# Where the heads' queries, keys and values are loaded in an attention period: loads with places of their own, SP's order written out, products placed later

## The chip, the cores and the metric

One core of a Trainium2 chip runs the kernel. The metric is device time in microseconds for one execution. The engines are TensorE (PE in the rows; its weight loads are PEld), VectorE (DVE), ScalarE (ACT), GpSimd (POOL) and SyncE (SP). SP does no arithmetic; it issues DMA transfers, and so does ScalarE here. A `q` behind an engine's name is its sequencer, which waits and issues.

## The reference, cut to what matters

One layer of a hybrid decoder, in float32: RMSNorm, one input projection, three groups of heads, a gate, an output projection, a residual and a last RMSNorm. The change touches the attention of the prompt, 2048 positions:

```python
for win, dil in ((128, 1), (512, 4), (2048, 16)):      # 8 heads of 64
    s = q @ k / 8 - slope * dil * dist                 # inside the dilated window
    p = exp(s - max(s)); l = sum(p); o = p @ v / l
attn_o = merge of the three o, weighted by their denominators
mem_o  = softmax(mq @ mk / 8) @ mv                     # 4 heads, 256 memory tokens
```

The kernel takes one maximum per position and head over all three windows, so that the three sums and products can be added up without a further weighting.

## The kernel before, in words

Queries and keys were projected earlier and lie in scratch memory as a high and a low part (`dq_hi`, `dq_lo`, `dk_hi`, `dk_lo`), so that float32 products are made of exact pieces. Values lie in the output `p_v`.

The attention is a chain of twelve units: eight `Head`s (0 to 7) and four `MemHead`s. Each has two halves. `scores` loads the unit's keys (`ks`, two loads of 512 KB) and queries (`qh`, `ql`, four loads of 512 KB, `q_load`) and, for a `Head`, its values in three layouts (`v1`, `v2`, `v3`, 512 KB each). It then makes the score blocks in 24 steps (six for a memory head): two products of `qk` per block on TensorE, the bias added on the way out of PSUM by VectorE (`biased`, L791), maxima by `mx.add` (L735). ScalarE regroups the keys by residue before steps 0 and 16 (`regroup`, `kr`, L814). The score tiles are S3, SS (also called S1) and S2.

`Maxima.finish(half)` ends each half of the maxima. TensorE transposes them (L742), VectorE reduces (`mc`, L744), a DMA stores 4 KB to the scratch `dmax` (L745), and a second one loads them back, spread over 128 partitions, as one half of `Rm`, 512 KB (L746). The load must wait until the store has landed. Both DMAs go out on ScalarE's queue. `finish(0)` is called at step 22 of a head's `scores`, `finish(1)` in its `values`.

`values` subtracts Rm from the scores on GpSimd (L911, L912, L917, L932, L933), takes exponentials on ScalarE (L913, L914, L918, L934, L936), multiplies by the values on TensorE into `acc` (`pv`, L906), and sums the weights (`Sums.add`, L759). `finish_head` turns the sums into reciprocals, spreads them with two groups of transposes (L771, L780; `rx`, L774), multiplies `osb` by them (L781) and stores it to `dmix` (L784, two stores of 256 KB).

`period` runs the scores of unit i+1 beside the values of unit i. `values` is a generator that yields places: a place p is taken at the first step k with k/24 not below p, a place above 1.0 in the next period. `with tc.manual_schedule(engines={PE})` keeps TensorE's program order as written in the seven periods of full heads; the order on the other engines, SP's queue among them, is found by the planner of the framework, which starts an instruction when it believes it ready and lets `high_priority(350)` go ahead of others. So in the kernel before the loads, written at the head of `scores`, are issued when the planner finds their buffer free.

Buffers: keys, queries and values of a unit lie in pools `keys[turn]` and `vals[turn]`, by the unit's parity, one set each. Those of turn 1 take the place of the rows and weights of the projection (`p0`), which `z_last`, the last of the gate's projection, runs with beside unit 0's scores. PSUM banks are shared by rings: `psP` 0 and 1, `psQ` 2 and 3 (scores), `psT` 4 and 5 (transposes).

Of the kernel before, what the change touches and what calls it, by code (L numbers as in the profile page):

```python
# [8 lines left out]
F = mybir.dt.float32  # L9
R = mybir.dt.float32r  # L10
# [9 lines left out]
T = 2048  # L20
NS = 32
NR = T + NS
H = 8
# [4 lines left out]
SLOPE = [2.0 ** -(h + 1) for h in range(H)]  # L28


def f32(ap):
    return ap.bitcast(F)


def ap_of(x, off, dims):
    return bass.AP(tensor=x.tensor, offset=x.offset + off, ap=dims)
# [238 lines left out]
def tile_step(ctx, tc, x_prompt, x_sample, mem_prompt, ck, cv, cconv, cmk, cmv, g_in, w_in, conv_w,  # L275
              g_mem, w_mem, w_out, g_final,
              y_p, y_s, p_k, p_v, p_cv, p_mk, p_mv, s_k, s_v, s_cv):
    nc = tc.nc
# [18 lines left out]
    psP, psQ, psT = Ring((0, 1)), Ring((2, 3)), Ring((4, 5))  # L297
# [5 lines left out]
    dk_hi = dr.tile([512, T], F, name="dk_hi")  # L303
# [393 lines left out]
    def z_last():  # L697
        for ct in range(8 - ZL, 8):
            yield from z_proj(ct, "A")
# [21 lines left out]
    parts_ = [None, None]  # L721
    dmax = [dr.tile([64, 32], F, name="dmax%d" % i) for i in range(2)]

    class Maxima:


# [10 lines left out]
        def finish(self, half):  # L737
            sl = slice(32 * half, 32 * half + 32)
            m = wk.tile([128, 32], F, name="mx")
            nc.vector.tensor_reduce(m, self.parts[:, sl, 0:self.n], axis=AX.X, op=OP.max)  # L740
            pt = psT.tile([128, 4, 128], F, name="pt")
            nc.tensor.transpose(pt[:32, 0], m, ident)  # L742
            mc = wk.tile([32, 32], F, name="mc")
            nc.vector.tensor_reduce(mc, pt[:32, 0].rearrange("p (q c) -> p c q", q=4), axis=AX.X, op=OP.max)  # L744
            nc.scalar.dma_start(self.d[sl], mc)  # L745
            nc.scalar.dma_start(self.Rm[:, 1024 * half:1024 * half + 1024], ap_of(self.d, 1024 * half, [[0, 128], [1, 1024]]))  # L746

    class Sums:

# [12 lines left out]
    def finish_head(o_sb, sums, row, at):  # L762

        rx = wk.tile([128, 16, 64], F, name="rx", bufs=1)
        ls = rx[:, 0:8].rearrange("p (a b) c -> p a (b c)", a=4)
        nc.scalar.activation(ls.rearrange("p a (J b) -> p a J b", b=8),
                             sums.ps.rearrange("p x y -> p (x y)").rearrange("p (J a b) -> p a J b", a=4, b=8), AF.Copy)
        yield at
        pt = psP.tile([128, 4, 128], F, name="pp")
        for a in range(4):  # L770
            nc.tensor.transpose(pt[:, a], ls[:, a], ident)  # L771
        rl = wk.tile([128, 16], F, name="rl")
        nc.vector.reciprocal(rl.rearrange("p (a g) -> p a g", g=4), pt[:, :, 0::32])
        nc.scalar.activation(rx, rl.unsqueeze(2).to_broadcast([128, 16, 64]), AF.Copy)  # L774
        for k in range(2):
            yield at + 0.06 + 0.03 * k
            pb = psP.tile([128, 4, 128], F, name="pp")
            for i in range(4):
                c = 8 * k + 2 * i
                nc.tensor.transpose(pb[:, i], rx[:, c:c + 2].rearrange("p a e -> p (a e)"), ident)  # L780
            nc.vector.tensor_mul(o_sb[:, 4 * k:4 * k + 4], o_sb[:, 4 * k:4 * k + 4], pb)  # L781
        for g in range(2):
            dst = dmix[row:row + 64, :T].rearrange("p (r g b) -> p g r b", g=2, b=128)[:, g]
            nc.sync.dma_start(dst, o_sb[g * 64:(g + 1) * 64])  # L784
# [8 lines left out]
    class Head:  # L793


        def __init__(self, h, turn):
            self.h, self.turn = h, turn

        def scores(self):
            h, sl = self.h, -SLOPE[self.h]  # L800
            kp, vp = keys[self.turn], vals[self.turn]
            ks = kp.tile([128, T], R, name="ks")
            nc.sync.dma_start(f32(ks[0:64]), dk_hi[h * 64:(h + 1) * 64])
            nc.sync.dma_start(f32(ks[64:128]), dk_lo[h * 64:(h + 1) * 64])
            qh, ql = q_load(h * 64, self.turn)

            kr = kp.tile([128, T], R, name="kr")

# [6 lines left out]
            regroup(16, 4)  # L815
            qh4 = qh.rearrange("p (r u) -> p r u", r=4)
            ql4 = ql.rearrange("p (r u) -> p r u", r=4)
            v1 = vp.tile([128, 16, 64], F, name="v1")
            v2 = vp.tile([128, 4, 4, 64], F, name="v2")
            v3 = vp.tile([128, 16, 64], F, name="v3")  # L820
            vsrc = p_v[0, 0, :, h, :]
            nc.sync.dma_start(v3, vsrc.rearrange("(b r) e -> b r e", r=16))
            for r4 in range(4):
                nc.sync.dma_start(v2[:, r4], vsrc.rearrange("(j k r) e -> r k j e", r=4, k=128)[r4])
            nc.sync.dma_start(v1, vsrc.rearrange("(j k) e -> k j e", k=128))
            self.v = v1, v2, v3

            Rm = vp.tile([128, T], F, name="Rm")
            S3 = vp.tile([128, 4, 16, 32], F, name="S3")
# [65 lines left out]
        def values(self):  # L895
# [23 lines left out]
            weights3(0)  # L919
            for r4 in range(2):  # L920
                weights2(r4)
            yield 0.08
            self.mx.finish(1)
            weights3(1)
            for r4 in range(2, 4):
# [20 lines left out]
            def products3(rh):  # L946
                for a in range(4):
                    for g in range(2):
                        r = 4 * a + 2 * rh + g
                        pv(rh, g, po4[:, rh, a], v3[:, r], S3[:, 2 * rh + g, :, 8 * a:8 * a + 8])  # L950
            yield 0.50
            products2(0)
            yield 0.57
            products3(0)
            yield 0.61
            products3(1)
            for g in range(4):
                sums.add(g, 0, 512, S3[:, g].rearrange("p J c -> p (J c)"))
            yield 0.70
            products2(1)  # L960
            yield 0.75
            for g in range(4):
                sums.add(g, 0, 512, S2[g][:, :, 0:4].rearrange("p j J c -> p j (J c)"))
            for g in range(4):
                sums.add(g, 128, 384, S2[g][:, 0:3, 4:8].rearrange("p j J c -> p j (J c)"))
            for jq in range(4):
                yield 0.80 + 0.08 * jq
                for j in range(4 * jq, 4 * jq + 4):
                    m = 2 if j < 15 else 1
                    for rh in range(2):  # L970
                        for g in range(2):
                            pv(rh, g, po[:, rh, 32 * j:32 * j + 32 * m], v1[:, j],
                               S1[:, j, 2 * rh + g, 0:m].rearrange("p J c -> p (J c)"), last=(j == 15))
            o_sb = wk.tile([128, 8, 128], F, name="osb", bufs=1)
            o_v = o_sb.rearrange("p (a r) (J b) -> p r a J b", r=2, b=8)
            for rh in range(2):
                nc.scalar.activation(o_v[:, rh], po4[:, rh], AF.Copy)
            yield 1.08
            for g in range(4):
                sums.add(g, 32, 480, S1[:, 0:15, g, 1])  # L980
            for g in range(4):
                sums.add(g, 0, 512, S1[:, :, g, 0], last=True)
            yield from finish_head(o_sb, sums, 256 + self.h * 64, 1.17)

    class MemHead:
        def __init__(self, h, turn):
            self.h, self.turn = h, turn

        def scores(self):
            h, vp = self.h, vals[self.turn]  # L990
            qh, ql = q_load(512 + h * 64, self.turn)
            mk = keys[self.turn].tile([128, T], R, name="ks").rearrange("p (a b) -> p a b", b=128)[:, 0:2]
            nc.sync.dma_start(f32(mk[0:64]).rearrange("p a b -> p (a b)"), dmk_hi[h * 64:(h + 1) * 64])
            nc.sync.dma_start(f32(mk[64:128]).rearrange("p a b -> p (a b)"), dmk_lo[h * 64:(h + 1) * 64])
            Rm = vp.tile([128, T], F, name="Rm")
            mx = Maxima(self.turn, Rm, 2)
            S = {}
            for hf in range(2):
                for kb in range(2):
                    S[kb, hf] = vp.tile([128, 8, 128], F, name="S", bufs=4)  # L1000
                for q in range(2):
                    for kb in range(2):
                        ps = psQ.tile([128, 4, 128], F, name="qk")
                        c = 1024 * hf + 512 * q
                        qk(ps, mk[:, kb], qh[:, c:c + 512], ql[:, c:c + 512])
                        nc.scalar.activation(S[kb, hf][:, 4 * q:4 * q + 4], ps, AF.Copy)  # L1006
                    yield
                for kb in range(2):
                    mx.add(mx.parts[:, 32 * hf:32 * hf + 32, kb], S[kb, hf].rearrange("p r (x c) -> p (r x) c", c=32))
            self.S, self.Rm = S, Rm.rearrange("p (r b) -> p r b", b=128)  # L1010
            for hf in range(2):
                mx.finish(hf)
                yield
# [36 lines left out]
    streams = []  # L1050
# [13 lines left out]

    def period(scores, n, values):

        for x in streams:
            x[0] -= 1.0
            x[2] += 1.0
        streams.append([0.0, values, 0.0])  # L1070
        for i in range(n):
            advance(i / n)
            with tc.high_priority(350):
                next(scores, None)
        with tc.high_priority(350):
            for _ in scores:
                pass
        advance(1.0)

    units = [Head(h, h % 2) for h in range(H)] + [MemHead(h, h % 2) for h in range(HM)]  # L1080
    interleave(units[0].scores(), z_last(), 24, 3 * ZL)
    p0.close()
    vals[1] = ctx.enter_context(tc.tile_pool(name="vals1", bufs=1, reuse_waits="tile"))
    keys[1] = p2q.enter_context(tc.tile_pool(name="keys1", bufs=1, reuse_waits="tile"))
    with tc.manual_schedule(engines={mybir.EngineType.PE}):
        for i in range(H - 1):
            period(units[i + 1].scores(), 24, units[i].values())
    for i in range(H - 1, len(units) - 2):
        period(units[i + 1].scores(), 6, units[i].values())
    advance(9.0)  # L1090
    with tc.high_priority(350):
        for _ in units[-1].scores():
# [161 lines left out]
```

## Time and profile before

| | us |
|---|---|
| median of 3 runs | 1436.53 (1435.77 to 1441.44) |
| profiled execution, its own time | 1437.99 |
| its span in the trace | 1436.2 |
| TensorE busy | 1260.9 (88%) |
| VectorE, ScalarE, GpSimd busy | 644.6, 441.9, 457.1 |

The span is from the first to the last instruction; a time within it is counted from its start. Busy times are sums over the whole span. Matmuls are pipelined, so TensorE's busy share is no measure of how well it is used.

### The profile page before, as it was taken

The page shows a single profiled execution, that of the slowest core. Times are in us where ns is not written, and L with a number is a line of the kernel's source. Part 1 is how long each engine was busy: PE and PEld are TensorE (multiplying, and loading weights), DVE is VectorE, ACT ScalarE, POOL GpSimd, SP SyncE. Part 2 cuts the span into 40 slices and gives each one's busy share as a digit, 9 for nine tenths or more (in the row PEclk, how much of TensorE's full clock was granted, in tenths as well). Part 3 has the DMA queues.
Part 4 walks back from the last instruction along what each step waited for, and adds up shares of the span by engine and source line. Part 5 has one row for each costly group of instructions (what it writes and reads, how often), then busy time and mean ns, then how long its engine had stood idle before and what let it go on. Part 6 is the DMA issues. An engine that isn't in the chain of part 4 may idle for free. (4 is left out here: it accounts for less than half of the span.)

```text
span 1436.2 us, 20119 instructions
## 1 busy us (share of the span) xinstructions
PE 1260.9 (88%) x7814; PEld 1000.3 (70%) x7814; DVE 644.6 (45%) x1201; ACT 441.9 (31%) x692; POOL 457.1 (32%) x398
## 2 busy tenths in 40 slices
PE   7999999997989999999999277778887687899998
PEld 5778989887878867678879265556655332578886
DVE  4554212566657213006303365667666225454442
ACT  4433123223330000111222145555544366411211
POOL 2120001555455001116400055455566374200000
PEclk9999999999999999999999688999989889999999
DMA  6442224678884264865463946687643755766541
GB/s 220 143 150 88 82 95 147 203 237 248 272 271 136 75 154 145 194 187 154 149 157 85 208 104 149 147 177 177 142 108 82 175 127 172 220 211 196 184 147 73
DMA packets 228103, 229.57 MB, mean 160 GB/s; under 512 B 67348, under 2 KB 182280, under 8 KB 223912
## 3 DMA queue, kind: packets, MB, share of 16 engines
q1 hardware_dynamic: 211880, 194.62, 50.4%
q10 hardware_dynamic: 16128, 33.66, 6.8%
q8 instruction: 62, 1.02, 0.3%
q14 instruction: 33, 0.27, 0.1%
HBM read 171.92 MB, written 56.31 MB: 159 GB/s over the span
## 5 line engine op out<-in xcount | busy, mean ns | idle before, releaser
L359 PE MATMUL b<-hA_hi,whi 128*128 128x384 f32 (+1 forms) x576 | 192.5, 334 | 16.4 <-ACT big L607 10.7
L359 PE MATMUL b<-hA_hi,wlo 128*128 128x384 f32 (+1 forms) x576 | 190.1, 330 | 0.0
L359 PE MATMUL b<-hA_lo,whi 128*128 128x384 f32 (+1 forms) x576 | 189.7, 329 | 0.0
L351 POOL TENSOR_TENSOR wlo<-wraw,whi 128x512 fp32r<-128x512 f32 x56 | 80.9, 1463 | 293.5 <-ACT whi L350 293.5
L359 PE MATMUL b<-hB_hi,whi 128*128 128x512 f32 (+1 forms) x416 | 162.9, 392 | 7.9 <-DVE vt L476 2.2
L124 POOL TENSOR_TENSOR spr<-sk,sqb 128x512 f32<-128x512 f32 (+2 forms) x110 | 121.2, 1112 | 130.1 <-DMA sk<-in_cache_win_k_dram 45.3
L359 PE MATMUL b<-hB_lo,whi 128*128 128x512 f32 (+1 forms) x416 | 162.5, 391 | 0.0
L359 PE MATMUL b<-hB_hi,wlo 128*128 128x512 f32 (+1 forms) x416 | 161.8, 389 | 0.0
L359 PEld LDWEIGHTS b<-hA_hi,whi 128*128 128x128 f32 x576 | 111.3, 193 | 22.6 <-ACT big L607 11.8
L125 DVE TENSOR_REDUCE sc<-spr 128x8 f32<-128x512 f32 (+1 forms) x160 | 88.3, 571 | 75.2 <-POOL spr L124 74.8
L791 DVE SCALAR_TENSOR_TENSOR S<-dt,b 128x128 f32<-128x128 f32 (+2 forms) x224 | 69.9, 351 | 99.6 <-PE b L788 68.1
L359 PEld LDWEIGHTS b<-hA_hi,wlo 128*128 128x128 f32 x576 | 111.3, 193 | 4.1 <-issue 3.3
L917 POOL TENSOR_TENSOR S<-S,Rm 128x512 f32<-128x512 f32 x32 | 40.1, 1276 | 230.4 <-DMA Rm<-dmax 198.9
L359 PEld LDWEIGHTS b<-hA_lo,whi 128*128 128x128 f32 x576 | 111.2, 193 | 2.9 <-issue 2.9
L787 PE MATMUL b<-qh,kr 128*128 128x256 f32 x256 | 76.4, 324 | 35.1 <-DMA qh<-dq_hi 30.3
L1157 PE MATMUL b<-woh,mh 128*128 128x512 f32 x256 | 102.3, 404 | 4.4 <-ACT mh L1148 4.3
L1157 PE MATMUL b<-woh,ml 128*128 128x512 f32 x256 | 102.2, 401 | 0.1
L1157 PE MATMUL b<-wol,mh 128*128 128x512 f32 x256 | 101.2, 400 | 0.0
L906 PE MATMUL acc<-S,v 128*64 128x128 f32 (+1 forms) x512 | 64.7, 373 | 40.6 <-ACT S L913 31.3
L409 POOL TENSOR_TENSOR ss<-ss,nhalf 128x1 f32<-128x1 f32 (+1 forms) x34 | 19.6, 578 | 251.7 <-DVE ss L408 246.4
L359 PEld LDWEIGHTS b<-hB_hi,whi 128*128 128x128 f32 x416 | 78.8, 189 | 25.6 <-issue 3.6
L735 DVE TRANSPOSE_TENSOR_REDUCE mparts<-S 128x12 f32<-128x384 f32 (+1 forms) x96 | 76.5, 825 | 44.6 <-ACT S L1006 44.3
(234 smaller groups left out, 2379.4 us busy)
## 6 DMA issues: line engine op xcount, KB each, us to landing
sk<-in_cache_win_k_dram SPq DMA_DIRECT2D x72, 256.0 KB, 4.3
vq<-in_cache_win_v_dram SPq DMA_DIRECT2D x36, 512.0 KB, 4.3
wraw<-in_w_in_dram SPq DMA_DIRECT2D x48, 256.0 KB, 3.7
sqb<-dqs SPq DMA_DIRECT2D x48, 256.0 KB, 4.1
qh<-dq_hi SPq DMA_DIRECT2D x24, 512.0 KB, 8.6
ql<-dq_lo SPq DMA_DIRECT2D x24, 512.0 KB, 9.1
Rm<-dmax ACTq DMA_DIRECT2D x24, 512.0 KB, 13.5
v<-out_dram SPq DMA_DIRECT2D x16, 512.0 KB, 12.6
```

What stands on the lines that cost most here:

```text
L124: E.tensor_mul(pr[:n, :width], kt, qt)
L125: nc.vector.tensor_reduce(dst, pr[:n, :width].rearrange("p (h e) -> p h e", e=64), axis=AX.X, op=OP.add)
L351: lo_eng.tensor_sub(lo[:, a:a + 4], raw, f32(hi[:, a:a + 4]))
L359: nc.tensor.matmul(ps, a(d), b(d), start=(n == 0), stop=(n == 23))
L409: nc.gpsimd.tensor_tensor(ss[:n], ss[:n], nhalf[:n], op=OP.pow)
L735: nc.vector.tensor_reduce(out, scores, axis=AX.X, op=OP.max, apply_transpose=True)
L787: nc.tensor.matmul(out, keys, a, start=True, stop=False)
L791: nc.vector.scalar_tensor_tensor(S, dt, sl, ps, op0=OP.mult, op1=OP.add)
L906: nc.tensor.matmul(out[g * 64:(g + 1) * 64], lhsT, rhs, start=(rh, g) not in started, stop=last, skip_group_check=True)
L917: nc.gpsimd.tensor_sub(S3[:, r4], S3[:, r4], mr[:, r4])
L1157: nc.tensor.matmul(self.ps[k], l[:, d], r[d][:, sl], start=first and i == 0, stop=last and i == 2)
```

## The change

The loads leave `scores` for methods of their own, `load_qk` and `load_v`. A new generator `loads(n)` gives them places in period n, which runs the scores of unit n beside the values of unit n−1: queries and keys of unit n+1 at 0.2, values of unit n at 0.4. Unit 0's loads and unit 1's queries and keys are issued before the periods. SP's order is kept as written in the periods of full heads, beside TensorE's. The two DMAs of the maxima go from ScalarE's queue to SP's. Several places in `values` move: the first products from 0.50 to 0.60, the others between 0.01 and 0.08 later, `finish_head`'s two multiplications to 0.12 and 0.16 behind its own place. The scores get a third PSUM bank, the transposes keep one. `period` does its bookkeeping at its end and not at its start.

```diff
+    psQ, psT = Ring((2, 3, 4)), Ring((5,))
...
-            nc.scalar.dma_start(self.d[sl], mc)
-            nc.scalar.dma_start(self.Rm[:, 1024 * half:1024 * half + 1024], ap_of(self.d, 1024 * half, [[0, 128], [1, 1024]]))
+            nc.sync.dma_start(self.d[sl], mc)
+            nc.sync.dma_start(self.Rm[:, 1024 * half:1024 * half + 1024], ap_of(self.d, 1024 * half, [[0, 128], [1, 1024]]))
...
-            yield at + 0.06 + 0.03 * k
+            yield at + 0.12 + 0.04 * k
...
+        def load_qk(self):
+            h, kp = self.h, keys[self.turn]
+            self.ks = kp.tile([128, T], R, name="ks")
+            nc.sync.dma_start(f32(self.ks[0:64]), dk_hi[h * 64:(h + 1) * 64])
+            nc.sync.dma_start(f32(self.ks[64:128]), dk_lo[h * 64:(h + 1) * 64])
+            self.q = q_load(h * 64, self.turn)
+
+        def load_v(self):
...
+            nc.sync.dma_start(v3, vsrc.rearrange("(b r) e -> b r e", r=16))
+            for r4 in range(4):
+                nc.sync.dma_start(v2[:, r4], vsrc.rearrange("(j k r) e -> r k j e", r=4, k=128)[r4])
+            nc.sync.dma_start(v1, vsrc.rearrange("(j k) e -> k j e", k=128))
...
-            yield 0.08
+            yield 0.1
             self.mx.finish(1)
...
-            yield 0.50
+            yield 0.60
             products2(0)
-            yield 0.57
+            yield 0.65
             products3(0)
-            yield 0.61
+            yield 0.68
             products3(1)
...
-            yield 0.70
+            yield 0.77
             products2(1)
-            yield 0.75
+            yield 0.80
...
-                yield 0.80 + 0.08 * jq
+                yield (0.84, 0.91, 0.97, 1.05)[jq]
...
-            yield 1.08
+            yield 1.12
...
-            yield from finish_head(o_sb, sums, 256 + self.h * 64, 1.17)
+            yield from finish_head(o_sb, sums, 256 + self.h * 64, 1.2)
...
+    units[0].load_qk()
+    units[0].load_v()
     interleave(units[0].scores(), z_last(), 24, 3 * ZL)
...
-    with tc.manual_schedule(engines={mybir.EngineType.PE}):
-        for i in range(H - 1):
-            period(units[i + 1].scores(), 24, units[i].values())
-    for i in range(H - 1, len(units) - 2):
-        period(units[i + 1].scores(), 6, units[i].values())
+    units[1].load_qk()
+
+    def loads(n):
+
+        yield 0.2
+        units[n + 1].load_qk()
+        yield 0.4
+        units[n].load_v()
+
+    def periods(first, last, n):
+        for i in range(first, last):
+            streams.append([0.0, loads(i), 0.0])
+            period(units[i].scores(), n, units[i - 1].values())
+    with tc.manual_schedule(engines={mybir.EngineType.PE, mybir.EngineType.SP}):
+        periods(1, H, 24)
+    periods(H, len(units) - 1, 6)
```

## Rows read from the trace of the kernel before

**Rows 1.** The page's second part: the span in 40 slices, busy tenths.

```profile
PE   7999999997989999999999277778887687899998
...
DMA  6442224678884264865463946687643755766541
```

**Rows 2.** Windows: length, busy us of each engine (instructions), clock, DMA share, GB/s.

```profile
860.50:902.94 42.44, 33.58 (x344) 24.03 (x342) 26.80 (x63) 21.95 (x27) 23.39 (x20) 0.88 0.70 150
...
801.50:830.20 28.70, 0.12 (x2) 0.04 (x1) 2.44 (x7) 10.39 (x11) 6.85 (x6) 0.50 1.02 223
...
822.00:830.00 8.00, 0.00 (x0) 0.00 (x0) 0.00 (x0) 6.48 (x7) 6.85 (x6) 0.50 1.03 213
...
1112.84:1222.60 109.76, 82.39 (x553) 37.90 (x552) 39.96 (x60) 57.21 (x86) 58.23 (x35) 0.86 0.63 160
```

**Rows 3.** TensorE's waits from 795 to 1112.8: total us, times, longest.

```profile
PE acc L906 <- ACT S L913: 31.3, 12, 4.8
PE b L787 <- DMA qh<-dq_hi: 28.6, 1, 28.6
PE b L780 <- ACT rx L774: 10.2, 6, 1.7
PE b L787 <- DVE SS L791: 6.9, 7, 1.0
PE b L787 <- DVE S L791: 6.5, 17, 0.9
```

**Rows 4.** SP's timeline: start, us, line, what it issues.

```profile
791.57 0.56 SPq L822 DMA_DIRECT2D v<-out_dram  x1
...
806.96 0.59 SPq L717 DMA_DIRECT2D qh<-dq_hi  x1
...
861.16 0.45 SPq L717 DMA_DIRECT2D qh<-dq_hi  x1
```

**Rows 5.** TensorE's timeline: start, us, line, operation, [idle before <- releaser].

```profile
830.19 0.55 PE L787 MATMUL b<-qh,kr 128*128 128x256 f32 x1 [28.58 <-DMA qh<-dq_hi]
832.50 0.56 PE L788 MATMUL b<-ql,kr 128*128 128x256 f32 x1 [1.76 <-DMA ql<-dq_lo]
...
851.50 1.73 PE L906 MATMUL acc<-S,v 128*64 128x256 f32 x16
...
860.50 0.27 PE L742 MATMUL b<-ident,mx 128*32 128x128 f32 x1
...
862.26 0.39 PE L787 MATMUL b<-qh,kr 128*128 128x256 f32 x1
...
877.11 0.28 PE L788 MATMUL b<-ql,ks 128*128 128x256 f32 x1
882.18 1.11 PE L906 MATMUL acc<-S,v 128*64 128x256 f32 x2 [4.79 <-ACT S L913]
884.36 3.25 PE L906 MATMUL acc<-S,v 128*64 128x256 f32 x14 [1.07 <-ACT S L913]
...
1112.84 0.28 PE L742 MATMUL b<-ident,mx 128*32 128x128 f32 x1
```

**Rows 6.** ScalarE's timeline: the maxima's stores and loads on its queue.

```profile
835.08 0.33 ACTq L745 DMA_DIRECT2D dmax<-mc  x1
...
836.44 0.33 ACTq L746 DMA_DIRECT2D Rm<-dmax  x1
...
861.79 0.37 ACTq L745 DMA_DIRECT2D dmax<-mc  x1
...
867.15 0.33 ACTq L746 DMA_DIRECT2D Rm<-dmax  x1
```

**Rows 7.** GpSimd's timeline: the first subtractions behind a maxima's load.

```profile
840.14 2.53 POOL L917 TENSOR_TENSOR S<-S,Rm 128x512 f32<-128x512 f32 x2 [10.53 <-DMA Rm<-dmax]
...
876.55 2.52 POOL L917 TENSOR_TENSOR S<-S,Rm 128x512 f32<-128x512 f32 x2 [19.83 <-DMA Rm<-dmax]
...
1141.95 2.48 POOL L917 TENSOR_TENSOR S<-S,Rm 128x512 f32<-128x512 f32 x2 [14.93 <-DMA Rm<-dmax]
```

More of the change, by code (lines that the diff above doesn't have):

```diff
@@ L797, in __init__ @@
             self.h, self.turn = h, turn
+        def load_qk(self):
[5 more added lines that the diff above has]
+        def load_v(self):
+            vp = vals[self.turn]
+            v1 = vp.tile([128, 16, 64], F, name="v1")
+            v2 = vp.tile([128, 4, 4, 64], F, name="v2")
+            v3 = vp.tile([128, 16, 64], F, name="v3")
+            vsrc = p_v[0, 0, :, self.h, :]
+            nc.sync.dma_start(v3, vsrc.rearrange("(b r) e -> b r e", r=16))
+            for r4 in range(4):
+                nc.sync.dma_start(v2[:, r4], vsrc.rearrange("(j k r) e -> r k j e", r=4, k=128)[r4])
+            nc.sync.dma_start(v1, vsrc.rearrange("(j k) e -> k j e", k=128))
+            self.v = v1, v2, v3
         def scores(self):
-            h, sl = self.h, -SLOPE[self.h]
+            sl = -SLOPE[self.h]
             kp, vp = keys[self.turn], vals[self.turn]
[L802 to L805, printed above, removed]
+            ks, (qh, ql) = self.ks, self.q
             kr = kp.tile([128, T], R, name="kr")
@@ L817, in scores @@
             ql4 = ql.rearrange("p (r u) -> p r u", r=4)
[L818 to L826, printed above, removed]
             Rm = vp.tile([128, T], F, name="Rm")
@@ L987, in __init__, with load_qk, load_v, scores @@
             self.h, self.turn = h, turn
[L989 to L992, printed above, removed]
+        def load_qk(self):
+            h = self.h
+            self.q = q_load(512 + h * 64, self.turn)
+            self.mk = mk = keys[self.turn].tile([128, T], R, name="ks").rearrange("p (a b) -> p a b", b=128)[:, 0:2]
             nc.sync.dma_start(f32(mk[0:64]).rearrange("p a b -> p (a b)"), dmk_hi[h * 64:(h + 1) * 64])
             nc.sync.dma_start(f32(mk[64:128]).rearrange("p a b -> p (a b)"), dmk_lo[h * 64:(h + 1) * 64])
+        def load_v(self):
+            pass
+        def scores(self):
+            vp, mk, (qh, ql) = vals[self.turn], self.mk, self.q
             Rm = vp.tile([128, T], F, name="Rm")
@@ L1065, in period @@
     def period(scores, n, values):
-        for x in streams:
-            x[0] -= 1.0
-            x[2] += 1.0
         streams.append([0.0, values, 0.0])
@@ L1078, in period @@
         advance(1.0)
+        for x in streams:
+            x[0] -= 1.0
+            x[2] += 1.0
     units = [Head(h, h % 2) for h in range(H)] + [MemHead(h, h % 2) for h in range(HM)]
+    units[0].load_qk()
+    units[0].load_v()
     interleave(units[0].scores(), z_last(), 24, 3 * ZL)
```

## The prediction

> **What bounds the kernel now.** I read the page first, for the slices. Of forty slices of 35.9 us, those before the twenty-third are at 9 tenths of TensorE or nearly so; that one falls to 2 with the transfer engines full, and the twelve behind it stay at 6 to 8 [rows 1]. The change touches only this stretch (from head 0's scores to the memory heads), so I took windows there. One period, from one `finish(0)` transpose on TensorE to the next, takes 42.44 us, in which TensorE is busy 33.58, VectorE 26.80, ScalarE 21.95, GpSimd 23.39 and the transfers 0.70 of the time; the granted clock is 0.88 on average, so part of it went at the lower of TensorE's two levels, 1.2 instead of 2.4 GHz [rows 2]. No engine is full, so it is a chain of waits. The six periods whose values run beside full scores go from 860.50 to 1112.84: 252.3 us, 42.06 each [rows 5].
>
> The waits of TensorE say what the chain is [rows 3]: 28.6 us once, for head 1's queries, and 31.3 us in twelve waits for exponentials of S2, two in each of the six periods. In the timeline these are the hole that ends at 830.19, and in a period a hole before the first product at 882.18, then 1.07 at 884.36 [rows 5].
>
> Behind the second hole stands the maxima's round trip. `finish(0)` issues its 4 KB store at 861.79, its 512 KB load Rm at 867.15, and GpSimd starts subtracting at 876.55: 14.8 us [rows 6, 7]. The same trip in a quiet stretch is 835.08, 836.44, 840.14: 5.1 us [rows 6, 7]. The difference is company: from 861.16 on SP issues four query halves of 512 KB and v1, 2.6 MB in all [rows 4]. The first hole is company too: from 791.57 SP issues v, then two units' keys and queries; the set that goes out last, from 806.96 on, is the one TensorE waits for [rows 4], in a stretch with the transfers at 1.02 [rows 2].
>
> **The change, part by part.** Nothing is computed more or less and no load is added. What moves is places.
>
> *Unit 1's keys and queries.* They are now issued ahead of all else that used to go at 791.57, and unit 2's only at 0.2 of period 1, v of unit 1 at 0.4. SP's order is fixed from period 1 on, so nothing of unit 2 can overtake. Six loads of 512 KB are 3.15 MB; at the 213 GB/s of 822 to 830 [rows 2] that is 14.8 us, and the fixed part of a load is 1.2 us (836.44 to 840.14 is 3.7, less 0.52 MB at that rate). So they land at about 791.6 + 16 = 807.6. TensorE went on at 830.19 and then lost 1.76 more for the second half [rows 5]; now near 809, allowing 1 us for spills of z between. Gain 21 us. Ends: 9.7 if they go out only behind head 0's `finish(0)`, 12 us later, 24 if nothing at all stands between (830.19 + 1.76 − 807.6).
>
> *The loads' places in a period.* Written order on SP is now: store and Rm of `finish(1)` at 0.1, queries and keys of the next unit at 0.2, the two dmix stores at 0.36, v at 0.4, then store and Rm of `finish(0)` at step 22. When head i's `finish(0)` comes, the 5.2 MB before it (3.15 + 0.52 + 1.57) were issued some 20 us earlier, and need 24.6 us at 213 GB/s. So Rm meets a quiet stretch, or the tail of v. I take the quiet 5.1 us and 1 us of tail: Rm is there 6 us after the store, 8.7 us sooner than now.
>
> *Products moved from 0.50 to 0.60.* A place is taken at the first of 24 steps not below it: 12 becomes 15. In the traced period the boundary (step 0) is 862.26 and step 11 ended at 877.4 [rows 5], so a step takes 1.26 us; three more are 3.8 us. The first product comes 5.6 us after GpSimd's start (876.55 to 882.18). With Rm 6 us after the store of 861.79 the exponentials are there at 873.4, before step 12, let alone 15. The wait of 5.2 us per period goes whole, and so does what the hole does to the clock: the sixteen products behind it take 882.18 to 887.6, less the 1.07 wait 4.3 us, where the same sixteen took 1.73 in the full-clock stretch at 851.50 [rows 5]: 2.6 us. Three more steps before the products are no loss in themselves; they are work that lay behind.
>
> *The other places.* `finish_head`'s two multiplications go from steps 6 and 7 to 8 and 9; the 1.7 us wait of TensorE for rx in each period [rows 3] is hidden behind three steps. *A third bank for scores* lets TensorE run one tile further ahead of VectorE: it waits 13.4 us for VectorE's bias in the window, some 2 per period [rows 3], of which I count half. One bank fewer for the transposes: in a head the two transposes are five steps apart, nothing; in a memory head they follow each other, and the second waits at most the 1.3 us from transpose to store (860.50 to 861.79) [rows 5, 6], four times, 5 us, inside the ±12 below. *Maxima's DMAs from ScalarE's queue to SP's*: 24 pairs of store and load, and the wait for the store between them, leave ScalarE's program; it is at 21.95 of 42.44 [rows 2] and not on the path, so zero. SP waits instead, 1.4 us [rows 6], with the next unit's loads behind it; they are done some 24 us into a period and due at its end. Without that slack the 1.4 us would count twice per period.
>
> Rm, on a queue of its own, needed 9.4 us from 867.15 to GpSimd's start in company and 3.7 alone [rows 6, 7]. The Trainium skill (DMA: Bandwidth & Descriptors, "Queues, rings and completion order") says that each transfer engine takes turns between the queues, of which SP and ScalarE have one each. By that rule Rm would have had half the engines, some 6 us, and to move it onto SP's queue is a loss, since there it stands behind all that SP has issued before. The trace does not bear out the half turn. By the row the sum below stands; by the rule it would be that of the first rival.
>
> *The new period.* Waits alone: 42.06 − 5.2 − 2.6 − 1.7 − 1 = 31.6. Floors: TensorE 33.58 − 3 of cold clock = 30.6; transfers 0.70 × 42.44 = 29.7 plus two stops for a store to land and Rm to start, 2 × 2, = 33.7. The transfers' floor is the higher. I take 33.5. Gain 8.6 × 6 = 51 us. Ends: 31 if only the waits for exponentials go, 69 at TensorE's floor.
>
> *Memory heads.* From 1112.84 to the first full run of output rows there are 109.8 us, TensorE busy 82.4 of them [rows 2], with holes of their own: GpSimd alone waits 14.93 us for one Rm at 1141.95 [rows 7]. SP's order there is still the planner's; the same loads fall due at the same ends of scores. I take zero, ends ±12.
>
> **Sum**: 1438.0 (this profiled execution; median 1436.5, so 1.5 above) − 21 − 51 = **1366 us**.
>
> **The rivals.**
> 1. *One queue becomes the bound.* 6.3 MB per period pass one queue in order, with two stops; if Rm keeps meeting the tail of v, lateness adds up until the products wait again, and the period settles at 36 to 38. For it: 29.7 us of transfer work in 33.5. Against: products at 0.60 have about 4 us to spare. 1438 − 21 − 6 × 5 = 1387 us.
> 2. *The memory heads pay back.* On SP, Rm there stands behind 2.1 MB of queries (10 us) in four heads. For it: such waits exist already [rows 7], which also speaks against it, since a queue of its own did not help. +25: 1391 us.
> 3. *Slower: Rm stands behind the period's loads.* If the maxima of `finish(0)` meet queries and v that are issued but not yet moved, 4.7 MB or 22 us, Rm arrives 25 us or more after step 0, and the period is Rm + 5.6 + 17 (42.4, less 19.9 to the first product, less 4.1 of wait and cold clock, less 1.4 for three steps that now lie ahead). It breaks even at Rm 19.5 us after step 0, or 23 with the first gain counted; at 25 the period is 47.6: 1438 − 21 + 6 × 5.5 = 1450 us. Against: the loads stand at 0.2 and 0.4, the maxima at 0.92.
> 4. *It does not do what it says.* The planner's order already hoists loads to the first moment a buffer is free; if unit 1's queries still go out late and the maxima still meet company, within 0.5%: 1436 us.
>
> **How the numbers follow.** Forecast (1345 to 1382) 0.63; rival 1 0.18; rival 2 0.09; rival 3 0.06; rival 4 0.04. Half a per cent is 7 us, about what a measurement here can tell from no change. Faster: 0.63 + 0.18 + 0.09 = 0.90; same 0.04; slower 0.06. The forecast's low end is TensorE's floor in most periods (1438 − 24 − 69 = 1345); rivals 1 and 2 reach to 1402. Range 1345 to 1402.
>
> **What would show it.** Right: no wait of 28 us for qh but one of about 8 at 801; the waits for S2's exponentials gone; six distances between `finish(0)` transposes of about 33.5; Rm to GpSimd's start 5 to 6 us; granted clock above 0.95 in a period; transfers above 0.85 of it. Rival 1: waits for exponentials of 1 to 4 us that grow from period to period, transfers near 1.0. Rival 2: the stretch behind the last full period longer than 110 us. Rival 3: GpSimd waiting 20 us or more for Rm. I would be wrong most likely in the period's new length: if more than half of VectorE's 26.8 us belongs to the first fifteen steps, VectorE sets the pace there and TensorE behind them, and the two parts add up to more than either floor.

## The result and the profile after

| | before | after |
|---|---|---|
| median, us | 1436.15 (4 runs, 1432.02 to 1441.44) | 1396.32 (4 runs, 1394.05 to 1399.11) |
| ratio | | 0.9722 (95%: 0.9684 to 0.9759) |
| span of the profiled execution | 1436.2 | 1395.7 |

The kernel is 39.8 us faster. The forecast was 70 us, the range 1345 to 1402. So the time lies in the range, but above the forecast's own band (1345 to 1382), and 30 us of the expected gain are missing.

The page's slices, TensorE and the transfers, after:

```profile
PE   6999999998988999999999937889887877899997
...
DMA  6443142677887255574545378776776856676541
```

The low slice of [rows 1] is still there, now the twenty-fourth and at 3 in place of 2. The slices behind it are at 7 to 9, so the periods are not tight. The windows (length, busy us and instructions of PE, PEld, DVE, ACT, POOL, then granted clock, DMA share, GB/s) cut the span at the same instructions as before, the resumption of TensorE and the `finish(0)` transposes:

```profile
820.42:851.88 31.46, 26.92 (x246) 20.79 (x246) 22.73 (x52) 15.35 (x18) 16.59 (x14) 0.88 0.75 160
851.88:1079.38 227.50, 189.25 (x2055) 146.64 (x2053) 163.31 (x373) 121.01 (x158) 140.75 (x120) 0.91 0.73 166
942.70:947.00 4.30, 4.30 (x20) 4.30 (x21) 2.65 (x4) 4.30 (x6) 4.30 (x5) 0.50 1.04 215
1079.38:1395.70 316.32, 281.19 (x1408) 197.40 (x1405) 137.85 (x180) 104.19 (x158) 77.18 (x57) 0.93 0.58 171
```

Against [rows 5] the 40.5 us of span divide like this. The first hole (TensorE's pause before unit 1's scores) ends at 820.42, 9.8 earlier. The first period takes 31.5 in place of 30.3, so 1.2 are lost. The six periods take 227.5 in place of 252.3, 37.9 each for 42.06: 24.8. The rest takes 316.3 in place of 323.4: 7.0. The granted clock in the periods is 0.91 and the transfers' share 0.73; the prediction had asked for 0.95 and 0.85.

TensorE's waits from 795 to 1092 (total us, times, longest), which answer to [rows 3]:

```profile
PE b L782 <- ACT rx L776: 34.5, 6, 6.0
PE b L789 <- DMA qh<-dq_hi: 20.3, 1, 20.3
PE b L789 <- DVE SS L793: 4.7, 5, 1.2
PE acc L915 <- ACT S L922: 1.4, 2, 1.1
```

The 31.3 us for exponentials are down to 1.4. In their place stand 34.5 us for rx, which had been 10.2: the old wait went and a new one, six times 5.75 us, came in. TensorE's and ScalarE's timelines in one period show what it is (start, us, operation, idle before and what ended it):

```profile
936.98 0.28 PE L790 MATMUL b<-ql,kr 128*128 128x256 f32 x1
942.70 1.12 PE L782 MATMUL b<-ident,rx 128*128 128x128 f32 x4 [5.44 <-ACT rx L776]
```

```profile
937.54 4.16 ACT L832 ACTIVATE kr<-ks 128x512 fp32r<-128x512 f32 x4
941.60 1.04 ACT L776 ACTIVATE rx<-rl 128x1024 f32<-128x1024 f32 x1
```

ScalarE isn't idle: before rx it makes the second grouping of the keys, four copies that take 4.16 us together and that nobody needs before step 16. That grouping overwrites the first, whose last reader is the product at 936.98. In the kernel before, the multiplications (L780) stood at steps 6 and 7, ahead of that reader in TensorE's written order, so the grouping could not be placed ahead of rx. At steps 8 and 9 they stand behind it, and the planner puts the grouping first. After the hole the clock is granted at 0.50, its lower level, from 942.70 to 947.00 (window above).

SyncE's and GpSimd's timelines show that the part of the prediction on Rm came true:

```profile
801.08 0.38 SPq L747 DMA_DIRECT2D dmax<-mc  x1
802.54 0.32 SPq L748 DMA_DIRECT2D Rm<-dmax  x1
802.96 0.48 SPq L804 DMA_DIRECT2D ks<-dk_hi  x1
...
928.62 0.33 SPq L747 DMA_DIRECT2D dmax<-mc  x1
930.05 0.34 SPq L748 DMA_DIRECT2D Rm<-dmax  x1
...
935.20 0.49 SPq L804 DMA_DIRECT2D ks<-dk_hi  x1
```

```profile
933.53 2.51 POOL L926 TENSOR_TENSOR S<-S,Rm 128x512 f32<-128x512 f32 x2 [13.26 <-DMA Rm<-dmax]
```

From the store at 928.62 to GpSimd's start there are 4.9 us, for 14.8 in [rows 6, 7]; the next unit's loads go out at 935.20, behind both pairs of maxima. At the first hole unit 1's keys go out only at 802.96, behind unit 0's maxima.

### The profile page after: what moved, and what is told of

The parts are those of the page before. It is cut to its first block, busy times and chain, and to the rows that moved or that the text cites. A ratio compares the mean times of both kernels' runs of the same rounds, so it can differ in the third digit from the quotient of the medians.

```text
span 1395.7 us, 20162 instructions
## 1 busy us (share of the span) xinstructions
PE 1247.1 (89%) x7814; PEld 1004.0 (72%) x7814; DVE 645.4 (46%) x1201; ACT 434.5 (31%) x692; POOL 458.1 (33%) x398
## 5 line engine op out<-in xcount | busy, mean ns | idle before, releaser
L359 PE MATMUL b<-hB_hi,whi 128*128 128x512 f32 (+1 forms) x416 | 164.5, 396 | 10.6 <-ACT big L607 2.0
L359 PEld LDWEIGHTS b<-hA_hi,whi 128*128 128x128 f32 x576 | 109.8, 191 | 20.4 <-ACT big L607 11.5
L359 PEld LDWEIGHTS b<-hB_hi,whi 128*128 128x128 f32 x416 | 79.6, 191 | 29.2 <-issue 3.4
L359 PEld LDWEIGHTS b<-hB_lo,whi 128*128 128x128 f32 x416 | 79.4, 191 | 19.9 <-issue 3.3
L359 PEld LDWEIGHTS b<-hB_hi,wlo 128*128 128x128 f32 x416 | 79.5, 191 | 18.3 <-issue 2.5
## 6 DMA issues: line engine op xcount, KB each, us to landing
v<-out_dram SPq DMA_DIRECT2D x16, 512.0 KB, 10.6
```

The lines of the kernel that those rows point to most:

```text
L359: nc.tensor.matmul(ps, a(d), b(d), start=(n == 0), stop=(n == 23))
```

## The experiments

The theory after the result: the missing gain in the periods is rx behind the copies on ScalarE, and the clock after that hole. The rival is the prediction's own first doubt: transfers, or VectorE in its first fifteen steps, set 37 us, and whatever stall is removed comes back elsewhere. All times in the table are windows between the same instructions, from one profiled execution of each kernel; "hole" is from the start of `z_last`'s last product on TensorE to the resumption, "rest" from the end of the six periods to the end of the span. The ratio is to the kernel before on the same chip, whose median there was 1438 to 1442 us.

| kernel | hole, us | first period | six periods (each) | rest | ratio (95%) |
|---|---|---|---|---|---|
| before | 38.8 | 30.3 | 252.3 (42.1) | 323.4 | 1 |
| after | 20.6 | 31.5 | 227.5 (37.9) | 316.3 | 0.9722 (0.9684–0.9759) |
| e1 multiplications at 6, 7 | 19.1 | 32.0 | 217.5 (36.3) | 313.5 | 0.9644 (0.9601–0.9687) |
| e2 rx first | 20.3 | 30.6 | 204.1 (34.0) | 308.7 | 0.9525 (0.9479–0.9571) |
| e3 two banks | 16.6 | 35.4 | 222.6 (37.1) | 311.7 | 0.9644 (0.9590–0.9698) |
| e4 maxima on ScalarE | 33.5 | 29.3 | 242.9 (40.5) | 312.0 | 0.9905 (0.9877–0.9934) |
| e5 rx first, two banks | 16.4 | 33.5 | 206.3 (34.4) | 316.1 | 0.9523 (0.9477–0.9570) |
| e6 rx first, z ahead | 16.7 | 41.6 | 206.4 (34.4) | 315.1 | 0.9559 (0.9510–0.9607) |
| e7 values' places alone | 38.9 | 31.4 | 242.5 (40.4) | 317.7 | 0.9894 (0.9851–0.9936) |
| e8 all but values' places | 19.6 | 32.3 | 241.7 (40.3) | 307.2 | 0.9722 (0.9682–0.9761) |
| e9 rx first, third bank later | 16.3 | 33.0 | 204.3 (34.1) | 306.4 | 0.9448 (0.9415–0.9481) |
| e11 order not written | 34.0 | 29.2 | 235.4 (39.2) | 314.0 | 0.9857 (0.9814–0.9899) |

**e1: the multiplications back at steps 6 and 7.**

```diff
-            yield at + 0.12 + 0.04 * k
+            yield at + 0.03 + 0.03 * k
```

> The changed kernel with one edit: the two multiplications by the row sums' reciprocals go back from steps 8 and 9 to steps 6 and 7 of the period, so that ScalarE's queue has rx ahead of the second regrouping of the keys again. Theory: TensorE's six waits for rx (34.5 us in the six periods of the changed kernel) come from rx standing behind four copies of the keys, and the half-speed clock behind each comes from the wait; the waits fall to about the 10 us of the kernel before, the period from 37.9 to 33 or 34 us, the time to 1365 to 1375 us. Rival: another engine or the transfers set 37 us a period anyway; the wait for rx goes and another of about its size takes its place (VectorE's places in SS or S, or queries), the time stays at 1388 to 1398 us.

Between the two: 36.3 us a period, and 0.9644, which is about 1385 us on the scale of the result (the median on its own chip, 1389.14, lies in the rival's range, but the kernel before took 1441.32 there). The waits for rx halve but stay at 3.0 us each, for another reason (waits of TensorE in the six periods, then ScalarE's timeline in one):

```profile
PE b L782 <- ACT rx L776: 18.0, 6, 3.5
PE b L789 <- DVE SS L793: 7.5, 8, 1.0
```

```profile
936.19 1.06 ACT L927 ACTIVATE S<-S 128x1024 f32<-128x1024 f32 x1 [1.66 <-POOL S L926]
937.42 0.31 ACT L923 ACTIVATE S<-S 128x128 f32<-128x128 f32 x1 [0.17 <-POOL S L920]
937.64 1.04 ACT L776 ACTIVATE rx<-rl 128x1024 f32<-128x1024 f32 x1
```

rx is ahead of the copies, but now exponentials stand ahead of it, the first of which waited 1.66 us for GpSimd. Rm comes so early that the exponentials are ready before rx. At the old place, TensorE meets that wait in full.

**e2: rx first, places kept.**

```diff
-        nc.scalar.activation(rx, ...)
+        last_rx.append(nc.scalar.activation(rx, ...).ins)
...
-            regroup(4, 4)
+            with tc.issue_after(last_rx[-1]) if last_rx else ExitStack():
+                regroup(4, 4)
```

> The changed kernel with its places kept (multiplications at steps 8 and 9), but the second regrouping of the keys made to stand behind rx in ScalarE's queue. Theory: it is the order on ScalarE and not the place of the multiplications; the waits for rx fall from 34.5 us to under 6, the period to 33 to 34 us, the time to 1360 to 1372 us, and no wait for the regrouped keys of over 1 us appears at step 16. Rival: the place is what matters, or the period has another bound; the time stays at 1388 to 1398 us, or TensorE now waits for the regrouped keys instead.

This one edit takes the period to 34.0 us. ScalarE's timeline, TensorE's waits in the six periods, and the window of the six:

```profile
932.24 1.04 ACT L778 ACTIVATE rx<-rl 128x1024 f32<-128x1024 f32 x1
933.18 4.29 ACT L834 ACTIVATE kr<-ks 128x512 fp32r<-128x512 f32 x4
...
940.08 4.05 ACT L834 ACTIVATE kr<-ks 128x512 fp32r<-128x512 f32 x4 [0.94 <-DMA ks<-dk_lo]
944.03 1.04 ACT L930 ACTIVATE S<-S 128x1024 f32<-128x1024 f32 x1
```

```profile
PE b L784 <- ACT rx L778: 12.8, 6, 2.6
PE acc L918 <- ACT S L930: 4.7, 5, 1.9
```

```profile
852.99:1057.04 204.05, 186.26 (x2054) 143.31 (x2052) 162.53 (x373) 121.54 (x158) 141.11 (x120) 0.96 0.81 186
```

The waits for rx fell to 12.8, not below 6 as the theory had it: as in e1, exponentials that wait for GpSimd stand ahead of rx. TensorE never waits for the regrouped keys. Some waits for exponentials came back (4.7 us): the exponential that TensorE waits for, at 944.03, stands behind four more copies, the first grouping of the next unit's keys, which the loads' new place has made ready. But VectorE works the same 162.5 us in 204 that it worked in 227.5, and the transfers run at 186 GB/s where they had run at 166: neither set the pace of the changed kernel. The rival is out. The six periods gave 23.4 us (227.5 − 204.1); the wait for rx alone is shorter by 21.7 (34.5 − 12.8).

**e3: two banks for scores, as before the change.**

```diff
-    psQ, psT = Ring((2, 3, 4)), Ring((5,))
+    psQ, psT = Ring((2, 3)), Ring((4, 5))
```

> The changed kernel with two banks for scores and two for transposes, as before the change. Theory: the third bank let unit 0's scores run ahead of the last z projection, whose end (798.9 us, 791.4 before) releases the memory of unit 1's queries and keys; with two banks their loads go out some 8 to 11 us earlier and ahead of the first half's maxima, and scores resume at 809 to 815 us in place of 820.4. In the periods two banks cost up to 1 us each, and rx stands behind two of the copies in place of four, which gives back some 2 us each: 1378 to 1390 us in all. Rival: the third bank has nothing to do with the first hole (resumed within 2 us of 820.4) and is worth 1 us or more a period: 1396 to 1404 us.

0.9644 of the time before is about 1385 us on the scale of the result: as the theory had it, and so is the hole's end at 813.39. The periods take 37.1 us, 0.8 less than in the change: only two of the four copies stand ahead of rx here. The last product of `z_last` on TensorE, with three banks (after) and with two:

```profile
799.85 0.29 PE L359 MATMUL b<-hA_lo,whi 128*128 128x288 f32 x1
```

```profile
796.84 0.29 PE L359 MATMUL b<-hA_lo,whi 128*128 128x288 f32 x1
```

And SyncE's queue with two banks:

```profile
798.55 0.48 SPq L804 DMA_DIRECT2D ks<-dk_hi  x1
```

With two banks unit 1's keys go out at 798.55, ahead of unit 0's maxima, and not at 802.96 behind them. With three, 96 of unit 0's score products stand ahead of `z_last`'s end in TensorE's order; with two, 56. The extra forty, at 0.12 us from start to start, are an estimated 4.9 us by which the memory for unit 1 comes free later; the two ends above are 3.0 apart in these two executions.

**e4: the maxima's transfers on ScalarE's queue, as before the change.**

```diff
-            nc.sync.dma_start(self.d[sl], mc)
-            nc.sync.dma_start(self.Rm[...], ...)
+            nc.scalar.dma_start(self.d[sl], mc)
+            nc.scalar.dma_start(self.Rm[...], ...)
```

> The changed kernel with the maxima's store and the load of Rm issued by ScalarE's queue again, as before the change; everything else as changed. Theory: what quieted Rm (4.9 us from the store to VectorE's partner's start in place of 14 and more) is the places of the loads, not the queue: Rm stays at 5 to 7 us, the periods at 37 to 38 us, and the first hole shortens by 2 to 4 us because unit 1's loads no longer stand behind unit 0's maxima: 1390 to 1396 us. Rival: the queue counts; on a queue of its own Rm takes 9 us or more again, the exponentials come late and each period loses 2 to 6 us: 1408 to 1432 us.

(The partner in the first sentence is GpSimd.) The rival held: the queue counts, by 15.4 us in the six periods. One period: SyncE's loads, ScalarE's queue, GpSimd.

```profile
952.90 0.44 SPq L717 DMA_DIRECT2D qh<-dq_hi  x1
...
954.68 0.59 SPq L718 DMA_DIRECT2D ql<-dq_lo  x1
```

```profile
953.36 0.33 ACTq L747 DMA_DIRECT2D dmax<-mc  x1
958.12 0.33 ACTq L748 DMA_DIRECT2D Rm<-dmax  x1
```

```profile
966.64 2.50 POOL L926 TENSOR_TENSOR S<-S,Rm 128x512 f32<-128x512 f32 x2 [19.51 <-DMA Rm<-dmax]
```

The queries now go out 0.5 us ahead of the store; in the changed kernel they go out at 936.41, 7.8 us behind it. The 4 KB store takes 4.8 us until Rm can go, Rm 8.5 us to GpSimd's start: 13.3, against 1.4 and 3.5 on SyncE's queue. So it is the order in one queue, not the places alone, that keeps Rm in a quiet stretch. Part of the loss comes another way: the load of Rm waits for the store in ScalarE's own program, and the last of the copies, and rx behind it, wait with it.

```profile
967.05 1.12 ACT L832 ACTIVATE kr<-ks 128x512 fp32r<-128x512 f32 x1 [2.38 <-DMA dmax<-mc]
```

TensorE waits 38.9 us for rx in the six periods, for 34.5 in the change; how the 15.4 us divide between the late Rm and this wait no run shows. Most of the rest of the loss is a hole of 33.5 us, 12.9 longer: with no maxima between, the planner put unit 2's keys and queries and unit 1's values ahead of unit 1's keys and queries, though SyncE's order was kept as written in the periods. Another 6.5 us lie ahead of the hole, where `z_last` ended later.

**e5: rx first with two banks.**

The edit of e2, and

```diff
-    psQ, psT = Ring((2, 3, 4)), Ring((5,))
+    psQ, psT = Ring((2, 3)), Ring((4, 5))
```

> The kernel with rx ahead of the second regrouping (the second experiment), with two banks for scores and two for transposes. It prices the third bank in periods without the long wait for rx. Theory: with two banks the first hole ends some 7 us earlier (813.4 in place of 820.4 us in the third experiment), and each period pays 1.5 to 2 us in waits of TensorE for VectorE's places in S and SS (18.2 us in the third experiment's six periods): periods of 35.5 to 36 us, and the ratio to the kernel before stays at 0.951 to 0.956. Rival: the third bank buys nothing in the periods: 34.0 us each, and the ratio falls to 0.945 to 0.949.

The hole is as the theory had it (resumption at 812.75), the periods nearly as the rival had it, 34.4; the ratio lies in the theory's range, but the longer periods that the theory put behind it are not there. Against e2 the third bank is worth 0.4 us a period, and 2.9 in the first one and 7.5 behind the last, and costs 9.6 in the resumption: 2.9 us in favour of the third bank by the spans, nothing by the ratios (0.9525 and 0.9523). In e3 the first period is longer too, by 3.9 us, but the rest is 4.6 shorter than after: what the bank does to the memory heads isn't settled by these two.

**e6: `z_last` ahead of unit 0's scores.** The edit of e2, and

```diff
             elif b:
-                b = next(second, "end") != "end"
+                with tc.high_priority(700):
+                    b = next(second, "end") != "end"
```

> The kernel with rx ahead of the second regrouping, three banks, and the steps of the last z projection given priority over unit 0's scores, so that unit 1's loads stand ahead of unit 0's first maxima. Theory: the end of the last z projection sets the end of the first hole; it comes some 8 us earlier, scores resume at 811 to 815 us in place of 822.4, the periods stay at 34 us, the ratio to before is 0.945 to 0.949. Rival: the landing of the queries is what the transfers at hand allow, whenever they are issued; scores resume after 819 us and the ratio stays at 0.951 to 0.954.

The hole closed as expected, at 814.02, and the ratio is worse than both ranges: the first period takes 41.6 us in place of 30.6. Unit 0's maxima are now transposed only behind unit 1's first scores on TensorE, their load goes out at 821.85, and the first exponentials come at 829.48.

```profile
818.91 0.41 PE L744 MATMUL b<-ident,mx 128*32 128x128 f32 x1
```

So the hole had hidden the time that unit 0's maxima need.

**e7: the kernel before with the values' new places alone.** All ten changed places of the diff, of which

```diff
-            yield at + 0.06 + 0.03 * k
+            yield at + 0.12 + 0.04 * k
...
-            yield 0.50
+            yield 0.60
```

> The kernel before with the later places of the values and of the multiplications alone; loads, queue, banks as before. Theory: the waits for exponentials (31.3 us in the kernel before) go, but the multiplications at steps 8 and 9 bring the order of ScalarE's queue in which rx stands behind the copies, 3 to 5 us a period, and Rm stays slow (9 us or more): periods of 41 to 43 us, ratio 0.99 to 1.01. Rival: later places alone are enough for the gain in the periods: 38 us each, ratio 0.975 to 0.985.

1.1% faster, nearer the theory than the rival, but not for its reasons. TensorE's waits for exponentials are 18 us shorter in the six periods, and some of that is given back, for the periods gain 9.8. The waits, and ScalarE's copies around rx in one period:

```profile
PE acc L906 <- ACT S L913: 13.3, 12, 1.6
PE b L780 <- ACT rx L774: 9.3, 6, 1.7
```

```profile
917.88 2.14 ACT L814 ACTIVATE kr<-ks 128x512 fp32r<-128x512 f32 x2 [1.49 <-PE b L788]
919.90 1.05 ACT L774 ACTIVATE rx<-rl 128x1024 f32<-128x1024 f32 x1
920.85 2.17 ACT L814 ACTIVATE kr<-ks 128x512 fp32r<-128x512 f32 x2
```

The waits for rx don't grow: with two banks the planner places two of the copies ahead of rx and two behind, here and in e3. All four stand ahead where the later places and the third bank come together. The loads' queue is as before, and so is the hole, 38.9 us.

**e8: the change without the values' new places.** The same ten lines, the other way:

```diff
-            yield at + 0.12 + 0.04 * k
+            yield at + 0.06 + 0.03 * k
...
-            yield 0.60
+            yield 0.50
```

> The changed kernel with all places of the values as before the change: loads, queue, order and the third bank alone. Theory: Rm lands within 5 us, so that the exponentials come some 9 us earlier and the products at their old places wait for them by 1 us a period or less, and rx stands ahead of the copies as before: periods of 34 to 36 us, ratio 0.953 to 0.965. Rival: the exponentials, 12 of them a half on GpSimd's pace, still come behind the old places; TensorE waits 2 to 5 us a period for S: 38 to 40 us, ratio 0.972 to 0.985.

The rival held, but for 0.3 us: 40.3 us a period. TensorE's waits in the six periods:

```profile
PE b L782 <- ACT rx L776: 22.2, 6, 5.1
PE acc L915 <- ACT S L922: 19.0, 5, 4.4
```

Rm is early, but the exponentials wait in ScalarE's order behind copies (at 956.48 one starts right behind the four of the next unit's first grouping), and rx behind exponentials, as in e1. In the six periods the two halves alone give 9.8 (e7) and 10.6 us (e8), together 24.8. The ratio of e8 is nevertheless that of the whole change, 0.9722: its rest is 9.1 us shorter than after, for a reason that no run shows. So by these traces the values' places are worth something in the periods only.

**e9: rx first, and the third bank only from unit 1 on.**

The edits of e5, and

```diff
     interleave(units[0].scores(), z_last(), 24, 3 * ZL)
+    psQ.ids, psT.ids = (2, 3, 4), (5,)
```

> The kernel with rx ahead of the second regrouping, with two banks for scores while unit 0 runs beside the last z projection and three from unit 1 on. Theory: the third bank is worth having only where no projection stands beside the scores; the first hole ends at 812 to 814 us as with two banks throughout (822.4 with three), the periods stay at 34 us and the memory heads at 308 to 310 us as with three: 8 to 10 us below the second experiment, ratio 0.944 to 0.948. Rival: what the hole gives back is paid in the first period (33.5 us in place of 30.6 with two banks) and by the later landing of Rm: ratio 0.949 to 0.953.

As the theory had it: resumption at 813.79, 34.05 us a period, 1357.71 us measured beside 1438.32 for the kernel before; the rest, 306.35, is a little less than its 308 to 310. This beats both kernels: 2.8% below the change by the two ratios.

```profile
846.83:1051.15 204.32, 185.02 (x2054) 138.79 (x2052) 161.20 (x373) 121.44 (x158) 141.03 (x120) 0.98 0.80 183
```

**e11: SyncE's order left to the planner.**

```diff
-    with tc.manual_schedule(engines={mybir.EngineType.PE, mybir.EngineType.SP}):
+    with tc.manual_schedule(engines={mybir.EngineType.PE}):
```

> The changed kernel without the written order of SyncE's queue: the loads keep their places in the program, the planner orders the queue. Now each head's loads stand ahead of the maxima of the head before, and unit 2's keys and queries ahead of unit 1's. Theory: the written order is what keeps Rm in front of the loads; without it Rm lands behind 2 to 4 MB of loads, 15 us or more after its issue or store, and the first hole ends 15 to 20 us later as it did with the maxima on ScalarE's queue: periods of 40 to 44 us, 1425 to 1450 us, ratio 0.99 to 1.01. Rival: loads issued early land early, so Rm meets a quiet queue and the order is worth nothing in the periods (37 to 39 us); only the first hole loses: ratio 0.975 to 0.985.

Between the two, nearer the rival: 39.2 us a period, and a hole of 34.0 for the theory's reason, unit 2's loads ahead of unit 1's. One period on SyncE's queue:

```profile
942.26 0.45 SPq L717 DMA_DIRECT2D qh<-dq_hi  x1
942.82 0.53 SPq L747 DMA_DIRECT2D dmax<-mc  x1
...
948.46 0.35 SPq L748 DMA_DIRECT2D Rm<-dmax  x1
```

The store stands behind the first of the four query loads, and Rm can go only 5.6 us later; Rm takes 8.4 us to land by the page's median, for 4.4 in the changed kernel. Written order is worth 7.9 us in the six periods and 13.4 in the hole.

## Why the prediction came out as it did, step by step

*Rm, and the products moved from 0.50 to 0.60.* Right. Predicted 6 us from store to GpSimd's start, measured 4.9; the waits for exponentials went from 31.3 to 1.4. By e7 and e8 neither the later places nor the loads with their order would have done it alone, and by e4 and e11 the queue and its written order both belong to it.

*The other places.* Here the prediction failed: "the 1.7 us wait of TensorE for rx in each period is hidden behind three steps". It grew to 5.75. The step took rx as a piece of work that starts when its input is there, and counted TensorE's steps ahead of its reader. But rx stands in ScalarE's queue, whose order the planner makes from the time at which it believes each instruction ready, and the moved reader released a competitor, the second grouping. e2 undoes that alone: 34.0 us a period, for 33.5 in the sum (which is 0.2 under the transfers' floor of 33.7 that the step itself had found). The six periods' term, 51 us predicted, was 24.8 in the change and 48.3 in e2.

*The closing doubt* (VectorE's first fifteen steps set the pace) and *rival 1* (one queue becomes the bound, 36 to 38 us, 1387) gave nearly the measured period by another mechanism. e2 and e9 exclude both for these periods: the same instructions go through VectorE in 204 us, and the same bytes through the queue. No rival had the wait for rx. So that the time lies in the range is luck in part: the range reaches to 1402 for the sake of rivals 1 and 2, and neither happened.

*Unit 1's keys and queries.* 21 us predicted, 9.8 measured. That is the step's lower end of 9.7, and nearly by its condition: the loads went out behind unit 0's maxima, at 802.96, 11.4 us later than the step had them; its sign, a wait for qh of about 8 us, was one of 20.3. From the end of `z_last` the hole shrank by 18.2 us (38.8 to 20.6), where the prediction had 791.4 to 809. But that end came 8.5 us later. 4.9 of these are the score products that the third bank lets ahead (e3): from the issue of unit 0's keys to the end of `z_last` it is 63.9 us after, 59.0 before and 60.5 in e3. The other 3.6 come earlier: unit 0's keys, issued in code that is the same in both, go out at 735.99 and had gone out at 732.37. e7 has that shift too (738.54 and a `z_last` that ends at 799.38), though its scores run with two banks. In the twelve traces they go out between 732.37 and 740.97, the kernel before being the earliest. So 3.6 us of this term are most likely a difference of the profiled executions and not of the change; with one trace of each kernel that isn't shown. The step's "nothing of unit 2 can overtake" held in the change only because the maxima stood in the same queue; in e4 unit 2's loads did overtake.

*A third bank.* Predicted 1 us of gain a period; 0.4 by e5 against e2, and the price beside `z_last` was not seen at all.

*Maxima's DMAs to SP's queue.* Counted as zero with a rule that spoke for a loss: the Trainium skill (DMA: Bandwidth & Descriptors, "Queues, rings and completion order") has the transfer engines take turns between queues. e4 shows that on ScalarE's queue, beside four query loads on SyncE's, Rm took 8.5 us, more than the 6 that the prediction had estimated for half the engines, and the store 4.8. So the trace does not bear out the half turn, as the prediction had said, nor the loss. The move was a gain of 15.4 us in the six periods: in the changed kernel's queue the loads stand behind the maxima and went out only at 935.20, when GpSimd had already started on Rm at 933.53. The zero also took ScalarE's wait for the store to be off the path; in e4 it holds rx back.

*Memory heads.* Zero ± 12 predicted. Of the 7.0 us that the rest gained, 3.1 lie in the prediction's stretch up to the first run of output rows, which starts at 1186.10: 106.7 us for 109.8. The other 3.9 lie behind it, in the output projection, which the change does not touch. Among the changed kernels above the rest varies from 306.4 to 317.7 us; what makes it so isn't settled. Rival 2 (they pay back 25 us, a stretch longer than 110) is out. So is rival 3 (Rm behind the loads) in the changed kernel: GpSimd waits 9.9 to 15.1 us for Rm in the six periods, where the rival had 20 or more.

## What to carry to other kernels

When a reader is moved on one engine, list what its move makes ready earlier on the engine that feeds it: where that engine's order is a planner's, the newly ready work may go ahead of what the reader waits for. A small round trip through memory that a chain hangs on did best here in the same queue as the bulk loads, ahead of them by written order; a queue of its own did not protect it (4.9 against 13.3 us). And a resource added to speed up one stage should be tried stage by stage: the third bank paid from unit 1 on, and beside the projection it cost about as much (e2, e5, e9).

## What the runs showed of the hardware

After a 4 KB store the load that waits for it could go 1.4 us later in a quiet stretch, 4.8 us later beside four 512 KB loads in another queue, the first of them issued 0.5 us before the store (e4), and 5.6 us later between such loads in the same queue (e11). A pause of 5.44 us of TensorE was followed by 4.3 us at a granted clock of 0.50, and the transposes behind it took 1.12 us for four where they take 0.66 in all six periods of e9. Behind stages that no edit touched, unit 0's keys went out up to 8.6 us apart in the profiled executions (732.37 to 740.97 us), which is as much as some terms of the sum.
